# A decoder block's prologue: the order of modulation sums, low parts, squares and loads on VectorE, ScalarE and the load queue

## The chip, the cores and the metric

The kernel runs on one core of one Trainium2 chip. The metric is the time of one execution in microseconds (us), as the device measures it. A core has TensorE (PE in the profile; its weight loads are PEld), VectorE (DVE), ScalarE (ACT), GpSimd (POOL) and SyncE (SP), which here only issues DMA loads. Each engine works through its own queue in order.

## The reference

One layer over 1024 tokens of 1024 channels, all in float32:

```python
mod = jax.nn.silu(c) @ w_ada + b_ada
shift, scale, gate = jnp.split(mod, 3, axis=-1)
h = rms_norm(x, norm_gain) * (1.0 + scale[:, None, :]) + shift[:, None, :]
proj = h @ w_in
q, k, v, z_a, u, z_b, m_a, m_b = jnp.split(proj, offs, axis=-1)
p_a = (stick_breaking_attention(q, k, v) * silu(z_a)) @ w_branch_a
p_b = (multiscale_causal_pool(u, pool_w, pool_scale) * silu(z_b)) @ w_branch_b
out = x + gate * ((sigmoid(m_a) * p_a + sigmoid(m_b) * p_b) @ w_out)
```

A final RMS norm follows. What matters here is the first part: the modulation (shift and scale) from `c`, the normalised and modulated `h`, and the projection `u`, whose weights are multiplied beforehand with the pooling maps `pool_w`.

## The kernel before

**Precision.** To multiply in something close to float32, most operands are held as two parts: a high part, rounded to the fast matmul type by a ScalarE cast, and a low part, the rest, from a VectorE subtraction. A product then takes three matmuls: high by high, high by low, low by high.

**The prologue, about the first 80 us.** It works on the first half of the tokens (four row blocks of x, `x0` to `x3`) and makes for each of the eight 128-channel blocks `kb` a column of `h`, transposed, while it also makes the weights of `u`.

- `norm_x(sb)` (L239): ScalarE squares a row block and sums it (`junk`), GpSimd takes the power -1/2 (`st`, L245), VectorE scales the row block.
- `modulation(kb)` (L262): VectorE multiplies a 1 MB block of `w_ada` (`wa`, three buffers) with silu(c), spread over all partitions (`scb`), in two instructions that also sum (`mj`, one for shift and one for scale; each is followed by a short read of the accumulator). Then `mods` adds the offsets: on VectorE for block 0, on ScalarE for the others.
- `turn_x(sh, kb)` (L283): four TensorE transposes of x into a PSUM bank (`xt`).
- `make_h(sh, kb)` (L288): ScalarE applies shift and scale (`hf`), casts the high part (`hT`), and VectorE subtracts for the low part (also `hT`).
- `mapped(g, q)` (L322): TensorE multiplies a quarter of `u`'s weights with the map of group g (`wm`; below m00 to m13 for g 0 and 1, m20 to m23 for g 2), ScalarE casts the high part, VectorE takes the low part (`wg`). For groups 0 and 1 the operands are plain float32; for 2 and 3 the operands are split first by `split_map` (`phl`) and `split_half` (`wt`).
- The loop over `kb` (L391): TensorE multiplies block `kb` of `h` with the finished weights into four, later six accumulators (`ua`): two matmuls each on the high part, then the transposes of block `kb + 2`, then one matmul each on the low part.

PSUM has eight banks in four pairs (`pj`, `z`, `av`, `tr`). The accumulators take the banks that m10 to m13 leave, and so wait for the low parts of these; m20 to m23 and the transposes share `av` and `tr`.

**What sets the order.** From L361 to L437 `pinned` is set, and each engine's instructions keep the order in which the program gives them. All of these pass through the helper `order` (L93), so that their line in the profile is L95. Loads by `load` (L230) keep their order on the SP queue in any case (L231); a load that reuses a buffer waits at the head of that queue, with all later loads behind it. After L437 (the rest of `u`, the second half's `h`, the values, the pooling branch) the builder chooses the order by its own estimate of times; the attention (from L800) is pinned again.

The order on VectorE in the loop is: both sums of block `kb + 2`, then, when ScalarE has made its high part from them, the low part of block `kb + 2`, then the sums of the next block.

Of the kernel before, what the change touches and what calls it, by code (L numbers as in the profile page):

```python
# [9 lines left out]
F32 = mybir.dt.float32  # L10
# [33 lines left out]
LOAD_WO = (0, 0, 0, 1, 1, 2, 2, 2)  # L44

WHOLE, G2 = 2, 1
EPS = 1e-6
WINDOWS = (2, 4, 8, 16)

# [4 lines left out]
def block_kernel(ctx, tc, a, out):  # L54
# [12 lines left out]
    def bank(tag, name):  # L67
        return psp.tile([P, 512], F32, tag=tag, bufs=BANKS[tag], name=name)
# [24 lines left out]
    def order(op):  # L93
        def issue(*args, **kw):
            ins = op(*args, **kw)  # L95
            if pinned[0]:
                tc.keep_in_program_order(ins)
        return issue
# [99 lines left out]
    with pool("init") as init:  # L198
# [9 lines left out]
        nc.sync.dma_start(crow, a["c_row"])  # L208
        scb = init.tile([P, D], F32, name="scb")

        crows = [bank("tr", f"crow{hf}") for hf in range(2)]
        for hf in range(2):
            mm(crows[hf], ones[0:1, :], crow[:, hf * 512:hf * 512 + 512], start=True, stop=True)

        def spread():
            for hf in range(2):
                sigb = init.tile([P, 512], F32, tag="hf", bufs=2, name=f"sigb{hf}")
                order(act.activation)(sigb, crows[hf], AF.Sigmoid)
                order(v.tensor_mul)(scb[:, hf * 512:hf * 512 + 512], crows[hf], sigb)
# [16 lines left out]
                xs.extend([pr[:, 0], pr[:, 1]])  # L236
            load(xs[sb], a["x"][sb * P:(sb + 1) * P, :])

        def norm_x(sb, meanwhile=None):  # L239
            st = init.tile([P, 4], F32, tag="st", bufs=4, name=f"st{sb}")  # L240
            junk = init.tile([P, D + 1], F32, tag="junk", bufs=1, name=f"junk{sb}")[:, :D + (sb < 4)]
            order(act.activation)(junk, xs[sb] if sb > 3 else xe[sb], AF.Square, scale=D ** -0.5, accum_out=st[:, 0:1])
            if sb > 3:
                gp.tensor_scalar(st[:, 0:1], st[:, 0:1], 1.0, EPS, op0=ALU.mult, op1=ALU.add)
            gp.tensor_tensor(st[:, 2:3], st[:, 0:1], mhalf[:, 0:1], op=ALU.pow)  # L245
            if meanwhile:
                meanwhile()

            for cl in ((slice(0, P), slice(P, D)) if sb in (2, 3) else (slice(0, D),)):
                order(v.tensor_scalar_mul)(xs[sb][:, cl], xs[sb][:, cl], st[:, 2:3])  # L250

        was = {}

        def load_mod(kb, parts=(slice(0, 2),)):
            if kb not in was:
                was[kb] = init.tile([P, 2, D], F32, tag="wa", bufs=3, name=f"wa{kb}")
            for i in parts:
                load(was[kb][:, i].rearrange("p k c -> p (k c)"), a["w_mod"][kb][:, i.start * D:i.stop * D])
# [3 lines left out]
        def modulation(kb, parts_=(0, 1)):  # L262
            wa = was[kb]
            if kb not in accs_m:
                accs_m[kb] = init.tile([P, 2], F32, tag="acc", bufs=2, name=f"acc{kb}")
            acc = accs_m[kb]
            for i in parts_:
                vj = init.tile([P, D], F32, tag="vjunk", bufs=1, name=f"mj{kb}_{i}")
                order(v.scalar_tensor_tensor)(vj, wa[:, i], 1.0, scb, ALU.mult, ALU.mult, accum_out=acc[:, i:i + 1])
                if kb == 0 and i == 0:  # L270
                    order(v.tensor_add)(mod[0][:, 0:1], acc[:, 0:1], bada_v[:, 0:1])
                elif kb == 0:
                    order(v.scalar_tensor_tensor)(mod[0][:, 1:2], acc[:, 1:2], gain_v[:, 0:1], affb[:, 0:1], ALU.mult, ALU.add)
                elif i == 0:
                    order(act.activation)(mod[kb][:, 0:1], acc[:, 0:1], AF.Identity, bias=bada_v[:, kb:kb + 1])
                else:
                    order(act.activation)(mod[kb][:, 1:2], acc[:, 1:2], AF.Identity, bias=affb[:, kb:kb + 1], scale=gain_v[:, kb:kb + 1])
            if parts_[-1] == 1:
                del was[kb]
# [3 lines left out]
        def turn_x(sh, kb):  # L283
            pt = xts[sh, kb] = bank(("tr", "av")[kb % 2], f"xt{sh}_{kb}")
            for i in range(4):
                transpose(pt[:, i * P:(i + 1) * P], xs[4 * sh + i][:, kb * P:(kb + 1) * P])

        def make_h(sh, kb, lo_eng):  # L288
            hf = init.tile([P, 512], F32, tag="hf", bufs=2, name=f"hf{sh}_{kb}")
            order(act.activation)(hf, xts.pop((sh, kb)), AF.Identity, bias=mod[kb][:, 0:1], scale=mod[kb][:, 1:2])  # L290
            sl = slice(sh * 512, sh * 512 + 512)
            order(act.copy)(h_hi[:, kb, sl], hf)
            order(lo_eng.tensor_sub)(h_lo[:, kb, sl], hf, h_hi[:, kb, sl].bitcast(F32))

        NA = 6
# [26 lines left out]
        def mapped(g, q, tag):  # L322

            if g not in wg:
                wg[g] = first.tile([P, 2, KB, 256], F32R, tag="wg", bufs=4, name=f"wg{g}")
            ps = bank(tag, f"wm{g}_{q}")
            th, ml = halves[g, q // 2], maps[g]
            for e in range(2):
                ks = slice((2 * q + e) % 4 * P, (2 * q + e) % 4 * P + P)

                pairs = [(th[:, cb, ks], ml[:, cb]) for cb in range(2)] if g < WHOLE else [
                    (th[:, i, cb, ks], ml[:, j, cb]) for i, j in ((0, 0), (0, 1), (1, 0)) for cb in range(2)]
                for n, (l, r) in enumerate(pairs):
                    mm(ps[:, e * 256:e * 256 + 256], l, r, start=n == 0, stop=n == len(pairs) - 1)

            def out():
                dst = wg[g][:, :, 2 * q:2 * q + 2].rearrange("p i k d -> p i (k d)")
                order(act.copy)(dst[:, 0], ps)
                order(v.tensor_sub)(dst[:, 1], ps, dst[:, 0].bitcast(F32))
            return out  # L340

        def parts(i):
# [15 lines left out]
        load_x(3)  # L358
        load_half(1, 1, t1[:, 1])
        load_mod(1)  # L360
        pinned[0] = True  # L361
        spread()
        outs = [mapped(0, 0, "pj")]
        outs.pop()()
        outs.append(mapped(0, 1, "pj"))
        norm_x(0)
        outs.pop()()
        mapped(0, 2, "z")()
        norm_x(1)
        mapped(0, 3, "z")()  # L370
        modulation(0, (0,))
        norm_x(2)
        mapped(1, 0, "pj")()
        modulation(0, (1,))
        outs.append(mapped(1, 1, "pj"))
        norm_x(3, outs.pop())
        outs.append(mapped(1, 2, "z"))
        turn_x(0, 0)
        make_h(0, 0, v)
        outs.append(mapped(1, 3, "z"))  # L380
        for out_ in outs:
            out_()
        turn_x(0, 1)
        modulation(1)
        make_h(0, 1, v)
        whl = {i: parts(i) for i in range(4)}
        accs = [bank(tags[i], f"ua{i}") for i in range(4)]
        h = (h_hi, h_lo)
        sl = slice(0, 512)

        for kb in range(KB):  # L391
            if kb + 2 < KB:
                load_mod(kb + 2)
            if kb == G2:
                load_map(2)
                for hf in range(2):
                    load_half(2, hf)
            new = kb == G2 + 3
            if new:
                for i in (4, 5):  # L400
                    whl[i] = parts(i)
                    accs.append(bank(tags[i], f"ua{i}"))
            todo = [(i, k) for i in range(len(accs)) for k in range(0 if i > 3 and new else kb, kb + 1)]
            for n, (i, k) in enumerate(todo):
                mm(accs[i], whl[i][0][:, k], h_hi[:, k, sl], start=k == 0, stop=False)
                mm(accs[i], whl[i][1][:, k], h_hi[:, k, sl], start=False, stop=False)
            if kb + 2 < KB:
                turn_x(0, kb + 2)
            for i, k in todo:
                mm(accs[i], whl[i][0][:, k], h_lo[:, k, sl], start=False, stop=k == KB - 1)  # L410
            if kb + 2 < KB:
                modulation(kb + 2)
                make_h(0, kb + 2, v)
            if kb == G2:
                split_map(2)
                for hf in range(2):
                    split_half(2, hf)
            if kb in (G2 + 1, G2 + 2):
                for q in (0, 1):
                    mapped(2, 2 * (kb - G2 - 1) + q, ("av", "tr")[q])()  # L420
            if kb == KB - 3:
                load_map(3)
                for hf in range(2):
                    load_half(3, hf)
                for sb in range(4, 8):
                    load_x(sb)
            if kb == KB - 2:
                split_map(3)
                for hf in range(2):
                    split_half(3, hf)  # L430
                for sb in range(4, 8):
                    norm_x(sb)
        for q in range(4):
            mapped(3, q, ("av", "tr")[q % 2])()
        for i in (6, 7):
# [520 lines left out]
```

## Time and profile before

| | |
|---|---|
| median of three runs | 1235.88 us (1234.64 to 1236.06) |
| the profiled execution | 1235.22 us, its span 1233.2 us |
| mean granted TensorE clock | 0.996 |
| TensorE busy | 1212.8 us, 98% of the span |
| VectorE, ScalarE, GpSimd busy | 797.6, 561.8, 202.4 us |

The profile is of one execution. The page gives busy time by engine, the timeline lists instructions with their start and length in us and, in brackets, the idle time of the engine before them and what ended it. A table by stretches gives busy us of each engine, the share of the clock that TensorE was granted (PEclk), the mean busy share of the 16 DMA engines and the rate of their transfers. A matmul's record lasts longer than its share of a stream of matmuls, since they overlap; the step from start to start is the cost in a stream.

### The profile page before, as it was taken

What the parts mean: (1) busy time and instruction counts of PE and PEld (TensorE: products, weight loads), DVE (VectorE), ACT (ScalarE), POOL (GpSimd) and SP (SyncE); (2) the same over time, 40 slices, a digit from 0 to 9 for tenths busy, and PEclk for the clock granted to TensorE, in tenths of its full rate; (3) what the DMA queues carried; (4) which work ended last, traced back from release to release, by engine and by line L of the source; (5) the groups of instructions that cost most, each with busy time, mean ns of one, the idle gap of its engine ahead of it and who ended that gap; (6) DMA issues with size and microseconds to landing.
All of it is one profiled execution on the core that took longest, in us unless ns stands there. A gap on an engine that the chain in (4) does not pass through costs nothing.

```text
span 1233.2 us, 16089 instructions
## 1 busy us (share of the span) xinstructions
PE 1212.8 (98%) x5760; PEld 1004.9 (81%) x5760; DVE 797.6 (65%) x1076; ACT 561.8 (46%) x1047; POOL 202.4 (16%) x365
## 2 busy tenths in 40 slices
PE   8899999999999999999999999999999999999997
PEld 5787888888888888888888888888888888888886
DVE  5644485476610297786878778688786863585654
ACT  4446333234301356566656556666666553232111
POOL 1010000000222342312313122222222310001001
PEclk9899999999999999999999999999999999999999
DMA  8635999425953321233423224231333225995612
GB/s 336 213 134 191 330 369 365 147 80 174 330 166 126 129 67 39 70 124 103 128 93 107 71 98 128 95 120 57 94 125 103 95 90 169 335 321 169 201 65 86
DMA packets 72803, 192.44 MB, mean 156 GB/s; under 512 B 7698, under 2 KB 21010, under 8 KB 70804
## 3 DMA queue, kind: packets, MB, share of 16 engines
q1 hardware_dynamic: 61956, 172.28, 40.7%
q10 hardware_dynamic: 10768, 19.14, 4.7%
q8 instruction: 45, 0.74, 0.2%
q14 instruction: 34, 0.28, 0.1%
HBM read 136.86 MB, written 50.34 MB: 152 GB/s over the span
## 4 chain that ended last, share of the span: by engine, by line
PE 83%; issue 6%; DVE 6%; POOL 2%; DMA 1%; ACT 1%; POOLq 0%; SPq 0%; DVEq 0%; ACTq 0%
PE p L95 27%; PE pb L95 7%; PE pa L95 7%; PE wzb L95 7%; PE v L95 7%; PE o L95 6%; PE u L95 4%; PE av L95 4%; PE z L95 4%; PE wt L95 4%; PE ua L95 2%; PE wm L95 2%; DVE om L689 2%; DVE be L690 2%; DMA gr<-ga_d 1%
## 5 line engine op out<-in xcount | busy, mean ns | idle before, releaser
L95 PE MATMUL p<-hT,w 128*128 128x512 f32 x1920 | 534.8, 399 | 0.3 <-ACT m_sg L184 0.3
L95 PEld LDWEIGHTS p<-hT,w 128*128 128x128 f32 x1920 | 341.5, 188 | 56.7 <-ACT m_sg L184 0.7
L689 DVE TENSOR_TENSOR_SCAN om<-om 128x512 f32<-128x512 f32 (+7 forms) x128 | 175.2, 1369 | 52.2 <-POOL om L687 29.0
L682 ACT ACTIVATE om<-z 128x512 f32<-128x512 f32 (+2 forms) x192 | 94.3, 491 | 103.8 <-PE z L95 101.9
L709 DVE TENSOR_TENSOR wt<-wt,wt 128x512 fp32r<-128x512 f32 (+1 forms) x160 | 100.9, 631 | 45.2 <-ACT wt L708 43.9
L687 POOL TENSOR_SCALAR_AFFINE_SELECT om<-om 128x128 f32<-128x128 f32 x128 | 67.5, 527 | 328.3 <-ACT om L682 302.2
L708 ACT CAST wt<-wt 128x512 fp32r<-128x512 f32 (+1 forms) x160 | 87.2, 545 | 68.6 <-PE wt L95 64.9
L690 DVE TENSOR_TENSOR be<-be,om 128x511 f32<-128x511 f32 (+7 forms) x128 | 101.6, 793 | 11.2 <-DVE om L689 0.9
L95 PEld LDWEIGHTS wt<-ident,be 128*128 128x128 f32 x576 | 72.0, 140 | 28.1 <-DVE wt L709 3.3
L95 PE MATMUL av<-wt,vv 128*128 128x512 f32 x320 | 94.2, 375 | 0.0
L683 ACT ACTIVATE be<-z 128x512 f32<-128x512 f32 (+2 forms) x192 | 93.6, 487 | 0.0
L95 PE MATMUL wt<-ident,be 128*128 128x128 f32 x576 | 89.1, 272 | 4.2 <-DVE wt L709 4.1
L95 PE MATMUL o<-wo,mhl 128*128 128x512 f32 (+2 forms) x408 | 90.2, 379 | 0.0
L95 PE MATMUL pa<-ga,wa 128*128 128x512 f32 x384 | 88.8, 389 | 0.0
L95 PE MATMUL pb<-gb,wb 128*128 128x512 f32 x384 | 87.2, 389 | 0.0
L95 PE MATMUL v<-wv,hT 128*128 128x512 f32 x384 | 87.2, 389 | 0.0
L95 PE MATMUL wzb<-hT,wzb 128*128 128x512 f32 x384 | 87.2, 389 | 0.0
L95 PEld LDWEIGHTS o<-wo,mhl 128*128 128x128 f32 x408 | 74.6, 188 | 14.1
L95 PEld LDWEIGHTS pa<-ga,wa 128*128 128x128 f32 x384 | 72.1, 188 | 14.9
L95 PEld LDWEIGHTS v<-wv,hT 128*128 128x128 f32 x384 | 72.1, 188 | 15.0
L95 PEld LDWEIGHTS wzb<-hT,wzb 128*128 128x128 f32 x384 | 72.1, 188 | 15.0
L95 PEld LDWEIGHTS pb<-gb,wb 128*128 128x128 f32 x384 | 72.1, 188 | 15.0
(124 smaller groups left out, 1430.6 us busy)
## 6 DMA issues: line engine op xcount, KB each, us to landing
w_raw<-in_w_in SPq DMA_DIRECT2D x40, 512.0 KB, 4.4
l_raw<-in_w_in SPq DMA_DIRECT2D x32, 512.0 KB, 5.7
wl_d<-l_raw SPq DMA_DIRECT2D x32, 512.0 KB, 4.0
w<-wl_d SPq DMA_DIRECT2D x32, 512.0 KB, 3.8
v_d<-vo SPq DMA_DIRECT2D x16, 512.0 KB, 5.5
vv<-v_d SPq DMA_DIRECT2D x8, 1024.0 KB, 5.6
wa_raw<-in_w_branch_a SPq DMA_DIRECT2D x16, 512.0 KB, 5.6
wa<-in_w_mod SPq DMA_DIRECT2D x7, 1024.0 KB, 4.9
```

The source lines that it names most:

```text
L95: ins = op(*args, **kw)
L682: act.activation(om[:, b0:b0 + n], zp[:, :n], AF.Sigmoid, scale=-0.125)
L683: act.activation(be[:, b0:b0 + n], zp[:, :n], AF.Sigmoid, scale=0.125)
L687: gp.affine_select(out=tl[:, :P], in_=tl[:, :P], pattern=[[1, P]], compare_op=ALU.is_gt, fill=fill, base=0, channel_multiplier=-1)
L689: v.tensor_tensor_scan(om[:, :W], om[:, :W], om[:, :W], 1.0, ALU.mult, ALU.min)
L690: v.tensor_mul(be[:, 1:W], be[:, 1:W], om[:, :W - 1])
L708: act.copy(wt[:, 0, :off], pt[:, :off])
L709: v.tensor_sub(wt[:, 1, :off], pt[:, :off], wt[:, 0, :off].bitcast(F32))
```

## The change

In the pinned prologue, the orders are rewritten:

- `norm_x` is parted into `square_x` and `scale_x`, and squares and scalings are placed one by one. The squares of x0 and x1 come before the casts of m00 and m02. Scaling and the sums of block 0 take other places among the low parts of m00 to m11.
- `make_h` can leave its low part to a new function `low_h`. Block 1's sums come in front of block 0's low part and of the low parts of m12 and m13; in the loop the sums of block `kb + 2` come in front of the low part of block `kb + 1`.
- Loads of `wa` are written behind the sums that free their buffer: block 2 before the pinned part, block 3 behind block 0's sums, followed by the loads of map 2, and block `kb + 5` behind the sums of block `kb + 2`. The loads of map 3 stand at `kb == 3` (were at 5), those of x4 to x7 at `kb == 6` (were at 5). The sequence of the loads among each other stays.
- Two matmuls of the ones by the identity (`BUSY = 2`) go into a PSUM bank that nobody reads, ahead of TensorE's first matmuls, which spread `c` over the partitions (`crow`).

The diff, cut to its core:

```diff
+        idle = bank("av", "idle")
+        for _ in range(BUSY):
+            mm(idle[:, :P], ones, ident, start=True, stop=True)
...
+        def low_h(sh, kb, lo_eng):
+            hf, sl = lows.pop(kb), slice(sh * 512, sh * 512 + 512)
             order(lo_eng.tensor_sub)(h_lo[:, kb, sl], hf, h_hi[:, kb, sl].bitcast(F32))
...
+        load_mod(2)
         pinned[0] = True
+        hi, lo_ = (0,), (1,)
         spread()
...
+        m00 = mapped(0, 0, "pj")
+        square_x(0)
+        m00(hi)
+        m00(lo_)
+        m01 = mapped(0, 1, "pj")
+        m01(hi)
+        scale_x(0)
+        m01(lo_)
+        m02 = mapped(0, 2, "z")
+        square_x(1)
+        m02()
+        scale_x(1)
+        m03 = mapped(0, 3, "z")
         modulation(0, (0,))
+        m03()
+        square_x(2)
+        m10 = mapped(1, 0, "pj")
+        m10(hi)
+        m11 = mapped(1, 1, "pj")
         modulation(0, (1,))
+        load_mod(3)
+        load_map(2)
+        for hf in range(2):
+            load_half(2, hf)
+        square_x(3)
+        scale_x(2, slice(0, P))
+        m10(lo_)
+        m11(hi)
+        scale_x(3, slice(0, P))
+        m11(lo_)
+        m12 = mapped(1, 2, "z")
         turn_x(0, 0)
+        scale_x(2, slice(P, D))
+        scale_x(3, slice(P, D))
+        make_h(0, 0, None)
+        m13 = mapped(1, 3, "z")
         turn_x(0, 1)
+        m12(hi)
         modulation(1)
+        load_mod(4)
+        low_h(0, 0, v)
+        m12(lo_)
+        m13(hi)
+        m13(lo_)
+        make_h(0, 1, None)
...
             if kb + 2 < KB:
                 turn_x(0, kb + 2)
+                modulation(kb + 2)
+                if kb + 5 < KB:
+                    load_mod(kb + 5)
+            if kb + 1 < KB:
+                low_h(0, kb + 1, v)
             for i, k in todo:
                 mm(accs[i], whl[i][0][:, k], h_lo[:, k, sl], start=False, stop=k == KB - 1)
             if kb + 2 < KB:
-                modulation(kb + 2)
-                make_h(0, kb + 2, v)
+                make_h(0, kb + 2, None)
```

More of the change, by code (lines that the diff above doesn't have):

```diff
@@ L46 @@
 WHOLE, G2 = 2, 1
+BUSY = 2
 EPS = 1e-6
@@ L237, in load_x, with square_x @@
             load(xs[sb], a["x"][sb * P:(sb + 1) * P, :])
-        def norm_x(sb, meanwhile=None):
-            st = init.tile([P, 4], F32, tag="st", bufs=4, name=f"st{sb}")
+        stats = {}
+        def square_x(sb):
+            st = stats[sb] = init.tile([P, 4], F32, tag="st", bufs=4, name=f"st{sb}")
             junk = init.tile([P, D + 1], F32, tag="junk", bufs=1, name=f"junk{sb}")[:, :D + (sb < 4)]
@@ L245, in norm_x, with scale_x @@
             gp.tensor_tensor(st[:, 2:3], st[:, 0:1], mhalf[:, 0:1], op=ALU.pow)
[L246 to L250, printed above, removed]
+        def scale_x(sb, cl=slice(0, D)):
+            order(v.tensor_scalar_mul)(xs[sb][:, cl], xs[sb][:, cl], stats[sb][:, 2:3])
         was = {}
@@ L292, in make_h @@
             order(act.copy)(h_hi[:, kb, sl], hf)
+            lows[kb] = hf
+            if lo_eng:
+                low_h(sh, kb, lo_eng)
+        lows = {}
+        def low_h(sh, kb, lo_eng):
+            hf, sl = lows.pop(kb), slice(sh * 512, sh * 512 + 512)
             order(lo_eng.tensor_sub)(h_lo[:, kb, sl], hf, h_hi[:, kb, sl].bitcast(F32))
@@ L334, in mapped, with out @@
                     mm(ps[:, e * 256:e * 256 + 256], l, r, start=n == 0, stop=n == len(pairs) - 1)
-            def out():
+            def out(which=(0, 1)):
                 dst = wg[g][:, :, 2 * q:2 * q + 2].rearrange("p i k d -> p i (k d)")
-                order(act.copy)(dst[:, 0], ps)
-                order(v.tensor_sub)(dst[:, 1], ps, dst[:, 0].bitcast(F32))
+                if 0 in which:
+                    order(act.copy)(dst[:, 0], ps)
+                if 1 in which:
+                    order(v.tensor_sub)(dst[:, 1], ps, dst[:, 0].bitcast(F32))
             return out
@@ L360, in block_kernel @@
         load_mod(1)
+        load_mod(2)
         pinned[0] = True
+        hi, lo_ = (0,), (1,)
         spread()
[L363 to L370, printed above, removed]
-        modulation(0, (0,))
-        norm_x(2)
-        mapped(1, 0, "pj")()
-        modulation(0, (1,))
-        outs.append(mapped(1, 1, "pj"))
-        norm_x(3, outs.pop())
-        outs.append(mapped(1, 2, "z"))
+        m00 = mapped(0, 0, "pj")
[11 more added lines that the diff above has]
+        m03 = mapped(0, 3, "z")
+        modulation(0, (0,))
+        m03()
[3 more added lines that the diff above has]
+        m11 = mapped(1, 1, "pj")
+        modulation(0, (1,))
+        load_mod(3)
[9 more added lines that the diff above has]
+        m12 = mapped(1, 2, "z")
         turn_x(0, 0)
[L379 to L382, printed above, removed]
+        scale_x(2, slice(P, D))
+        scale_x(3, slice(P, D))
+        make_h(0, 0, None)
+        m13 = mapped(1, 3, "z")
         turn_x(0, 1)
+        m12(hi)
         modulation(1)
-        make_h(0, 1, v)
+        load_mod(4)
[4 more added lines that the diff above has]
+        make_h(0, 1, None)
         whl = {i: parts(i) for i in range(4)}
@@ L391, in block_kernel @@
         for kb in range(KB):
[L392 to L397, printed above, removed]
             new = kb == G2 + 3
@@ L420, in block_kernel @@
                     mapped(2, 2 * (kb - G2 - 1) + q, ("av", "tr")[q])()
-            if kb == KB - 3:
+            if kb == 3:
                 load_map(3)
@@ L424, in block_kernel @@
                     load_half(3, hf)
+            if kb == KB - 2:
                 for sb in range(4, 8):
                     load_x(sb)
-            if kb == KB - 2:
                 split_map(3)
@@ L431, in block_kernel @@
                 for sb in range(4, 8):
-                    norm_x(sb)
+                    square_x(sb)
+                    scale_x(sb)
         for q in range(4):
```

## The prediction

> **What bounds the kernel now.** I read the page first, then busy time by stretches, the list of who waited for whom, the timeline of the first 80 us, and stretches again for the clock.
>
> ```profile
> span 1233.2 us, 16089 instructions
> ...
> PE 1212.8 (98%) x5760; PEld 1004.9 (81%) x5760; DVE 797.6 (65%) x1076; ACT 561.8 (46%) x1047; POOL 202.4 (16%) x365
> ```
>
> TensorE (PE) is busy 98% of the span, so an edit on other engines can only win where PE stands still or runs slowly. The stretches say where that is (us of the stretch, then busy us of each engine):
>
> ```profile
> core 0: us, PE busy (x) PEld busy (x) DVE busy (x) ACT busy (x) POOL busy (x), PEclk, DMA share, GB/s
> 0.00:10.00 10.00, 7.27 (x13) 4.03 (x14) 1.72 (x4) 2.69 (x4) 1.55 (x28) 1.00 0.75 266
> 10.00:25.50 15.50, 14.06 (x64) 11.97 (x63) 9.97 (x19) 9.48 (x17) 2.68 (x4) 1.00 0.98 381
> 25.50:33.00 7.50, 5.32 (x25) 3.83 (x24) 5.55 (x9) 2.67 (x6) 0.00 (x0) 0.97 0.91 340
> 33.00:40.00 7.00, 6.86 (x27) 4.97 (x26) 4.50 (x9) 2.83 (x7) 0.00 (x0) 0.79 0.52 178
> 40.00:50.00 10.00, 7.08 (x37) 6.41 (x38) 6.48 (x9) 6.31 (x11) 0.00 (x0) 0.83 0.41 134
> ```
>
> Between 10 and 50 us PE idles 1.44 + 2.18 + 0.14 + 2.92 = 6.7 us, and the granted clock drops. After that it has work all the time; the list of PE's waits from 80 to 420 us has one entry:
>
> ```profile
> PE u L95 <- ACT u_sg L191: 0.2, 1, 0.2
> ```
>
> So whatever brings PE sooner to where it is at 50 us should reach the end undiminished. What holds PE back is a loop through three engines, once per block (from the timeline):
>
> ```profile
> 31.36 0.69 DVE L95 TENSOR_TENSOR hT<-hf,hT 128x512 fp32r<-128x512 f32 x1 [1.91 <-ACT hT L95]
> ...
> 31.39 2.77 PE L95 MATMUL ua<-hT,wg 128*128 128x512 f32 x8 [2.18 <-ACT hT L95]
> 31.97 1.22 DVE L95 SCALAR_TENSOR_TENSOR mj<-wa,scb 128x1024 f32<-128x1024 f32 x1
> ...
> 33.23 1.23 DVE L95 SCALAR_TENSOR_TENSOR mj<-wa,scb 128x1024 f32<-128x1024 f32 x1
> ...
> 34.50 0.39 ACT L95 ACTIVATE mods<-acc,affb,vecs 128x1 f32<-128x1 f32 x1 [0.97 <-DVE mj L95]
> ...
> 34.92 0.78 ACT L95 ACTIVATE hf<-xt,mods 128x512 f32<-128x512 f32 x1
> 35.73 0.62 ACT L95 CAST hT<-hf 128x512 fp32r<-128x512 f32 x1
> 36.38 0.69 DVE L95 TENSOR_TENSOR hT<-hf,hT 128x512 fp32r<-128x512 f32 x1 [1.91 <-ACT hT L95]
> ```
>
> Low part (31.36), two modulation sums (31.97, 33.23), then ScalarE's three steps, then the next low part at 36.38: 5.02 us a block, of which VectorE (DVE) idles 1.91 because its next sums stand behind the low part that ScalarE has yet to feed. The clock follows PE's gaps:
>
> ```profile
> 10.00:12.00 2.00, 2.00 (x6) 1.64 (x5) 0.69 (x1) 1.63 (x3) 0.06 (x1) 1.00 1.07 410
> 14.00:16.00 2.00, 2.00 (x11) 1.75 (x10) 0.97 (x2) 1.30 (x2) 0.00 (x0) 1.00 1.03 418
> ...
> 22.36:25.77 3.41, 2.44 (x14) 2.19 (x15) 2.12 (x6) 2.04 (x4) 0.00 (x0) 1.00 0.83 308
> 29.18:32.60 3.42, 1.24 (x6) 1.04 (x6) 1.51 (x4) 1.78 (x3) 0.00 (x0) 1.00 0.77 256
> 32.60:36.01 3.41, 3.41 (x11) 2.74 (x11) 1.83 (x4) 1.74 (x4) 0.00 (x0) 0.50 0.57 156
> ...
> 42.84:46.25 3.41, 3.33 (x14) 3.04 (x15) 3.39 (x3) 0.94 (x1) 0.00 (x0) 0.50 0.23 94
> ```
>
> A stretch with PE busy 1.24 of 3.42 us is followed by one at 0.50; one with 2.44 of 3.41 is not. At the start the same matmuls go at 6 in 2 us around 11 us and 11 in 2 us around 15, so PE starts slow too.
>
> **The change, part by part.** *Prologue on DVE.* These rows carry it:
>
> ```profile
> 15.18 1.06 ACT L95 ACTIVATE junk<-x 128x1025 f32<-128x1025 f32 x1
> 15.31 0.69 DVE L95 TENSOR_TENSOR wg<-wm,wg 128x512 fp32r<-128x512 f32 x1 [1.03 <-ACT wg L95]
> ...
> 17.00 0.75 DVE L95 TENSOR_SCALAR x<-x,st 128x1024 f32<-128x1024 f32 x1 [0.99 <-POOL st L245]
> 17.66 0.68 DVE L95 TENSOR_TENSOR wg<-wm,wg 128x512 fp32r<-128x512 f32 x1
> ...
> 18.26 1.22 DVE L95 SCALAR_TENSOR_TENSOR mj<-wa,scb 128x1024 f32<-128x1024 f32 x1
> ...
> 19.86 1.03 POOL L245 TENSOR_TENSOR st<-st,mhalf 128x1 f32<-128x1 f32 x1 [1.18 <-ACT junk L95]
> ...
> 22.26 0.22 DVE L95 SCALAR_TENSOR_TENSOR mods<-acc,vecs,affb 128x1 f32<-128x1 f32 x1
> ...
> 23.33 0.33 PE L95 MATMUL xt<-ident,x 128*128 128x128 f32 x1 [1.44 <-DVE x L95]
> ...
> 26.96 1.21 DVE L95 SCALAR_TENSOR_TENSOR mj<-wa,scb 128x1024 f32<-128x1024 f32 x1
> ```
>
> The square of row block 1 (15.18) moves ahead of the third cast, into about 13.5; DVE's 0.99 wait before 17.00 goes. Walking the new queue by start-to-start steps (low 0.60, scaling 0.66, sum 1.25): low at 15.3, scaling 15.9, first sum 16.6 (was 18.26), low 17.9, second sum 18.5, its offset done at 20.0 (was 22.5). Then first part of x2, low, first part of x3 at 20.7 to 20.9 (20.9 if the GpSimd step again takes 1.03), low, the two rests, and block 1's first sum at 22.7 to 22.9, was 26.96: 4.2 us earlier. The transposes that waited 1.44 for x3 start at 21.4, as the matmuls ahead of them end. ScalarE's order from the third cast on is unchanged, so nothing there moves later. Its square of x0 now stands before the first cast, beside eight slow wm matmuls (2.7 us at 6 in 2 us) that the cast waits for anyway; should x0 land too late for that cover, the lateness is the cost.
>
> *New wait.* Low parts of the two last mapped tiles (m12, m13) now stand behind block 1's sums: 22.8 + 2 x 1.25 + low of h 0.60 + 0.69 = 26.6. PE has then issued the first two accumulators (24.9 by my walk) and idles about 1.6 us for the third's PSUM bank. It was not there before; it replaces the 1.44 and most of the 2.18.
>
> *The loop.* DVE's step is now two sums and a low part without the 1.91: 3.1 us. PE's is 12 matmuls of 0.23 (6.51 / 28, below) and 4 transposes of some 0.11 (at most 2.97 / 22, below), 3.2 us. So blocks 1 to 3 come at 3.2 instead of 5.0 us: block 1's matmuls at 28.9 (were 31.39), block 2's at 32.1, its low ones done at 35.3. Block 3's cast ends at 34.4: sums done 32.6, plus mods, hf, hT 1.9.
>
> *Map 2.* Splits keep their place behind that cast:
>
> ```profile
> 41.27 0.61 ACT L95 CAST phl<-praw 128x512 fp32r<-128x512 f32 x1
> ...
> 41.79 1.99 ACT L95 CAST wt<-wt_raw 128x1024 fp32r<-128x1024 f32 x2
> ...
> 42.86 2.36 DVE L95 TENSOR_TENSOR wt<-wt_raw,wt 128x1024 fp32r<-128x1024 f32 x2 [0.17 <-ACT wt L95]
> 42.88 4.82 PE L95 MATMUL wm<-phl,wt 128*128 128x256 f32 x24 [3.02 <-ACT wt L95]
> ...
> 50.90 3.09 PE L95 MATMUL wm<-phl,wt 128*128 128x256 f32 x24
> ...
> 53.82 6.51 PE L95 MATMUL ua<-hT,wg 128*128 128x512 f32 x28
> ```
>
> 34.35 + 0.52 + 1.04 gives 36.0 for the first half's high part: PE starts map 2 at 36.0, was 42.88, after 0.7 us of waiting instead of 3.02; four matmuls on it waits 0.8 for the half's low part (was 0.3). The 24 ran 4.82 us, mostly at half clock; at full clock 3.09, 1.7 less. Block 3 starts at 39.6, 8.0 us earlier. One us is given back: DVE must do block 4's sums (38.2 to 40.7) and a low part before it can lower m20, whose cast also follows block 4's on ScalarE (43.1); low at 43.8, while PE, done with block 3 at 42.8, wants that bank. The second 24 start at 43.9 instead of 50.90, and the 28 at 46.7 instead of 53.82: **7.1 us**. After that my walk finds margins of only 0.4 to 0.5 us (block 5's bank, m22's low part) but no wait; a miss costs about as much again.
>
> *Loads.* Their order on the SP queue is the same; only the release is earlier. The page's longest wait of that queue is for sums, and a 1 MB load takes
>
> ```profile
> wa<-in_w_mod SPq DMA_DIRECT2D x7, 1024.0 KB, 4.9
> ```
>
> 4.9 us from issue, or 2.75 at 381 GB/s back to back. Ten loads up to block 1's weights are 6.84 MB: 2.66 by 10 us (266 GB/s there), the rest by 21.0; block 2's by 23.7, block 3's by 26.5, map 2's by 29.9, block 4's by 32.7. Wanted at 22.8, 27.0, 30.1, 35 and 38.2: hidden, by 1.8 us at the closest. Gone by that cover, each us late is a us on DVE and on PE.
>
> *Two extra matmuls* on TensorE before the first: four passes of 128 columns, nearest row the transposes' 0.11, twice that at half clock, so 0.9 in all. They lie in PE's first idle 2.7 us (10.00 - 7.27), before the row of c lands, and can start only when their operands are made; bounds: nothing, or the whole 0.9 late. I take nothing, the nearer end, because the idle time is three times as long. A gain is a rival, below.
>
> *Clock.* My gaps of 1.6 and of 0.7 + 0.8 leave stretches of 3.4 us with PE busy 1.9, between the two rows that decide. I take full clock; a half-clock stretch would cost 0 around 30 us, where the walk has slack, and 0.8 to 1.3 around 40 to 45.
> [...]
>
> *Sum.* The profiled execution took 1235.2 (span 1233.2 and 2.0 around it); minus 7.1 is 1228.1. The median of the runs, 1235.88, lies 0.7 higher: **1228.8**.
>
> **The rivals.** *Earlier clock.* PE reports work from 2.73 us but is slow until about 12. If the extra full-array matmuls bring the release a 3.4 us stretch sooner, eight wm matmuls go at 0.22 instead of 0.43: 1.7 more, 1227.1. Against: 0.9 us is a quarter of a stretch.
> [...]
>
> *Half the gain.* Two half-clock stretches (2 us) and the two thin margins (1 us) leave 4: 1232. For: three short gaps close together. Against: the 2.44 row.
>
> *No change.* The DMA engines or a later stage absorb it: 1235 or so. Against: PE waits 0.2 us in 80 to 420; loads there start as buffers come free, so they move along.
>
> *Slower.* From line 437 the order is not pinned; the builder chooses it, and may choose anew after a changed prologue.
>
> ```profile
> 93.47 2.97 PE L95 MATMUL xt<-ident,x 128*128 128x128 f32 x22
> ```
>
> There eight blocks of transposes, each with hf, hT and a low part behind it (0.78 + 0.62 + 0.69 = 2.1 us), lie beside u matmuls. Were these issued first, eight blocks would wait 2.1 - 0.44 each, 13 us: 1242. It decides from five uncovered blocks on; the page shows every one covered today.
>
> **How the numbers follow.** Forecast 0.62, earlier clock 0.12, half the gain 0.14, no change 0.08, slower 0.04. About 0.2% (2.5 us) is what a measurement can tell from no change, so faster is 0.62 + 0.12 + 0.14 = 0.88, same 0.08, slower 0.04. The range takes in 1227.1 less the 1.4 us by which the runs differ, and the half gain: 1225.6 to 1232.0; outside it lie the last two and a tail.
>
> **What would show it.** Right: first sum of block 1 at about 22.8; DVE's waits for hT gone until the splits; PE waiting some 1.6 us near 25 and 1 us near 43; map 2 at 36 and 44; third map's matmuls at 69.4 instead of 76.5; granted clock 1.00 from about 12 on. Wrong: sums that wait for weights, half-clock stretches after 25 us, or new PE waits past 50 us.

## The result and the profile after

| | before | after |
|---|---|---|
| median | 1235.39 us (1234.64 to 1236.06, 4 runs) | 1228.06 us (1227.15 to 1228.42, 4 runs) |
| profiled execution, its span | 1235.22, 1233.2 us | 1228.19, 1226.2 us |
| mean granted clock | 0.996 | 0.999 |

The ratio is 0.994, with a 95% interval of 0.9922 to 0.9957: 7.3 us faster, where 7.1 were forecast (1228.8). When both kernels were measured once more, the ratio was 0.9936 (0.9922 to 0.9949).

The page of the profile after, to be held against the one before: TensorE (PE) does the same work and four matmul records more (x5764, was x5760); it is busy for 1.8 us less, in a span that is 7.0 us shorter.

```profile
span 1226.2 us, 16097 instructions
...
PE 1211.0 (99%) x5764; PEld 1003.3 (82%) x5764; DVE 796.8 (65%) x1076; ACT 561.7 (46%) x1047; POOL 202.8 (17%) x365
```

The stretches are those of the prediction:

```profile
0.00:10.00 10.00, 8.40 (x16) 4.95 (x17) 1.72 (x4) 2.78 (x5) 1.56 (x28) 1.00 0.74 250
10.00:25.50 15.50, 15.33 (x69) 12.64 (x67) 12.14 (x23) 9.97 (x20) 2.21 (x4) 1.00 1.02 410
25.50:33.00 7.50, 6.57 (x32) 5.27 (x33) 7.43 (x13) 4.68 (x11) 0.00 (x0) 1.00 1.02 407
33.00:40.00 7.00, 6.21 (x41) 5.13 (x40) 4.88 (x6) 3.97 (x6) 0.00 (x0) 1.00 0.53 215
40.00:50.00 10.00, 9.17 (x54) 7.76 (x53) 6.37 (x12) 5.81 (x11) 0.00 (x0) 1.00 0.82 305
```

PE's idle time between 10 and 50 us falls from 6.7 to 0.17 + 0.93 + 0.79 + 0.83 = 2.7 us, and in this execution the clock column reads 1.00 in all of these stretches (the last figure but two of each row), where the kernel before has 0.97, 0.79 and 0.83 between 25.5 and 50 us. VectorE (DVE) is busy 7.43 of the 7.5 us from 25.5 to 33, where it was busy 5.55: its queue no longer stands still there. The list of PE's waits in the first 80 us names the places that are left; its first entry is the start, ahead of the two extra matmuls:

```profile
PE idle L96 <- POOL x L232: 1.6, 1, 1.6
PE ua L96 <- DVE wg L96: 1.1, 1, 1.1
PE wm L96 <- DVE wg L96: 0.8, 1, 0.8
PE wm L96 <- DVE wt L96: 0.5, 1, 0.5
PE wm L96 <- ACT wt L96: 0.3, 1, 0.3
```

The other four are the waits of the forecast's walk, which has 1.6, 1.1, 0.8 and 0.7 us for them: the listed waits are 0.3 to 0.5 shorter. Most of that is the way of counting, since a record runs on past the issue of the next matmul (four `ua` matmuls take 1.17 us by their records and 4 x 0.23 in a stream). In the timeline the loop reads as follows; the columns are start, length, engine, line, operation, operands, count, and in brackets the idle time before.

```profile
22.67 1.22 DVE L96 SCALAR_TENSOR_TENSOR mj<-wa,scb 128x1024 f32<-128x1024 f32 x1
...
26.43 1.33 PE L96 MATMUL ua<-hT,wg 128*128 128x512 f32 x4 [1.08 <-DVE wg L96]
...
26.89 1.22 DVE L96 SCALAR_TENSOR_TENSOR mj<-wa,scb 128x1024 f32<-128x1024 f32 x1
...
28.15 1.23 DVE L96 SCALAR_TENSOR_TENSOR mj<-wa,scb 128x1024 f32<-128x1024 f32 x1
...
29.30 0.69 DVE L96 TENSOR_TENSOR hT<-hf,hT 128x512 fp32r<-128x512 f32 x1
...
29.90 1.22 DVE L96 SCALAR_TENSOR_TENSOR mj<-wa,scb 128x1024 f32<-128x1024 f32 x1
```

From sum to sum it is 29.90 - 26.89 = 3.0 us, with no idle time in between; it was 5.0. Behind the loop PE's timeline has the two halves of map 2 and the start of map 3:

```profile
35.80 0.74 PE L96 MATMUL wm<-phl,wt 128*128 128x256 f32 x4 [0.27 <-ACT wt L96]
...
43.71 3.08 PE L96 MATMUL wm<-phl,wt 128*128 128x256 f32 x24 [0.83 <-DVE wg L96]
...
69.41 3.02 PE L96 MATMUL wm<-phl,wt 128*128 128x256 f32 x24
```

The row of map 3 in the kernel before:

```profile
76.56 3.02 PE L95 MATMUL wm<-phl,wt 128*128 128x256 f32 x24
```

What the walk forecast and what the trace has, in us (the first row is an end, the others are starts):

| | before | forecast | after |
|---|---|---|---|
| offset of block 0's second sum done | 22.48 | 20.0 | 19.98 |
| block 1's first sum | 26.96 | 22.7 to 22.9 | 22.67 |
| map 2, first half | 42.88 | 36.0 | 35.80 |
| map 2, second half | 50.90 | 43.9 | 43.71 |
| first matmul of map 3 | 76.56 | 69.4 | 69.41 |

So 7.15 us are won by 70 us of 1226, and 7.0 are left at the end. From map 3 on all four computing engines issue the same instructions in the same order in both profiles, and PE's lead stays between 6.6 and 7.2 us. The order that the builder chooses has not changed, and no later stage took the gain back.

### The profile page after: what moved, and what is told of

It reads as the page before. It is cut to its first block, busy times and chain, and to the rows that moved or that the text cites. A ratio compares the mean times of both kernels' runs of the same rounds, so it can differ in the third digit from the quotient of the medians.

```text
span 1226.2 us, 16097 instructions
## 1 busy us (share of the span) xinstructions
PE 1211.0 (99%) x5764; PEld 1003.3 (82%) x5764; DVE 796.8 (65%) x1076; ACT 561.7 (46%) x1047; POOL 202.8 (17%) x365
## 4 chain that ended last, share of the span: by engine, by line
PE 81%; DVE 7%; issue 7%; POOL 2%; DMA 1%; ACT 1%; POOLq 0%; SPq 0%; DVEq 0%; ACTq 0%
PE p L96 29%; PE v L96 7%; PE pa L96 7%; PE pb L96 7%; PE o L96 6%; PE u L96 4%; PE wzb L96 4%; PE av L96 4%; PE wt L96 4%; PE z L96 4%; PE ua L96 2%; DVE om L727 2%; DVE be L728 2%; PE wm L96 1%; POOL om L725 1%
```

## The experiments

My theory (order theory): the gain is DVE's queue alone. In the prologue its sums come 4.2 us sooner, in the loop they no longer stand behind a low part that ScalarE has yet to feed. Rivals: the clock (the half-clock stretches of before are gone), the two extra matmuls, and the place of the loads. Within the prologue the moves were not tried one by one: how much of its part comes from the squares on ScalarE and how much from the sums on DVE is not shown by a run of its own.

**One part alone.** The loop's order put into the kernel before:

```diff
             if kb + 2 < KB:
                 turn_x(0, kb + 2)
+                modulation(kb + 2)
+            if kb > 0 and kb + 1 < KB:
+                low_h(0, kb + 1, v)
...
-                modulation(kb + 2)
-                make_h(0, kb + 2, v)
+                make_h(0, kb + 2, None)
```

> The kernel before, with the loop's order of the change alone: the sums of block kb + 2 stand ahead of the low part of block kb + 1; the prologue, the loads and the first matmuls are as before. Order theory (the gain comes from DVE's queue, part by part): block 1 still starts at 31.4 us, blocks 2 and 3 come sooner, because DVE no longer waits 1.9 us in front of the sums of block 3 and of block 4's neighbours; map 2 starts at about 40.5 instead of 42.9, its second half at 48.4 instead of 50.9: 2.6 us faster than before. Rival, clock theory (the gain is the half clock that goes away): PE still stands still 2.2 us before block 1, so one half-clock stretch stays, and the gain is what the other one cost, 1.7 us. Rival, loads or extra matmuls: 0.

Measured: 1232.02 us beside 1235.12, ratio 0.9974 (0.9963 to 0.9984): 3.1 us faster. The reverse, the change with the old order in the loop:

```diff
-        make_h(0, 1, None)
+        make_h(0, 1, v)
...
                 turn_x(0, kb + 2)
-                modulation(kb + 2)
-                if kb + 5 < KB:
-                    load_mod(kb + 5)
-            if kb + 1 < KB:
-                low_h(0, kb + 1, v)
...
-                make_h(0, kb + 2, None)
+                modulation(kb + 2)
+                if kb + 5 < KB:
+                    load_mod(kb + 5)
+                make_h(0, kb + 2, v)
```

> The change with the loop's order taken back: squares, scalings, sums and low parts up to the loop are as in the change, in the loop the low part of block kb + 2 stands behind the sums of that block, as before. Order theory: block 1's matmuls at 28.9 instead of 31.4 us, then the old step of 5.0 us a block, so map 2 starts at about 39.0 and its second half at 47.0: 4.0 us faster than before, and with the loop's 2.6 nearly the whole 7.1 (the rest, 0.5, is what the two do together). Rival, loop theory (only the loop's 1.9 us a block matter, what is won ahead of it is lost again in waits for weights): 0 to 1 us faster. Rival, clock theory: PE stands still over 3 us before map 2 as it did, so that half-clock stretch stays; the other one goes, 1.7 us.

Measured: 1231.40 us, ratio 0.997 (0.9959 to 0.9982): 3.7 us faster. PE's timeline with the loop's order alone, and then with the prologue's alone:

```profile
40.23 0.73 PE L95 MATMUL wm<-phl,wt 128*128 128x256 f32 x4 [0.52 <-ACT wt L95]
...
48.14 3.12 PE L95 MATMUL wm<-phl,wt 128*128 128x256 f32 x24 [0.84 <-DVE wg L95]
```

```profile
38.45 5.90 PE L96 MATMUL wm<-phl,wt 128*128 128x256 f32 x24 [3.00 <-ACT wt L96]
...
47.39 3.00 PE L96 MATMUL wm<-phl,wt 128*128 128x256 f32 x24
```

Map 2 starts where the order theory had it, within 0.6 us (40.5 and 39.0), and so does its second half (48.4 and 47.0). The parts nearly add up: 3.1 + 3.7 = 6.8 of 7.3 us.

In the second run's profile the clock does cost something. Map 2's first half ran at half clock (0.50 from 37.40 to 44.22 us), 5.90 us instead of 3.00. DVE's low part of m20, which the second half waits for in the other profiles, was done early enough:

```profile
45.74 1.28 DVE L96 TENSOR_TENSOR wg<-wm,wg 128x512 fp32r<-128x512 f32 x2
```

The first of the two ends at about 46.4, but PE, which had no idle time since 38.45, came to the second half only at 47.39, 0.9 us later. From half to half it is 8.9 us here, 7.9 in the run with the loop's order alone (8.0 in the kernel before). Map 3 starts 2.70 us sooner than before in the first run's trace and 3.58 in the second's, together 6.3 of the 7.15 of the change; 0.9 is what is missing.

**The clock by itself.** The kernel before, its clock kept up by extra matmuls in its two long waits:

```diff
             ps = bank(tag, f"wm{g}_{q}")
+            if (g, q) == (2, 0):
+                for _ in range(13):
+                    mm(ps[:, :P], ones, ident, start=True, stop=True)
...
+            if kb == 1:
+                warm = bank("av", "warm")
+                for _ in range(9):
+                    mm(warm[:, :P], ones, ident, start=True, stop=True)
```

> The kernel before, with extra matmuls of the ones by the identity, whose results are overwritten or never read, in PE's two long waits: 9 before block 1 (2.0 us) and 13 before map 2 (2.8 us). The granted clock should stay at 1.00 from 12 us on. Clock theory: the two half-clock stretches cost PE 1.7 us each, and at least the second of them counts, so 1.5 us faster than before or more. Order theory: after the second stretch PE waits for DVE's low part of m20, which stands behind block 4's sums whatever the clock, so map 2's first half ends 1.6 us sooner, PE waits that much longer before the second half at 50.9, and the time is as before within 0.3 us. This tells whether the 1.7 us that my sum booked under the clock was really in it.

Measured: 1235.48 us beside 1235.12, ratio 1.0002 (0.9993 to 1.001): no gain, and the interval leaves room for 0.9 us at most. The clock was kept (two stretches of this run; the clock is the third figure from the end), and PE's timeline says where the gain went:

```profile
41.83:45.24 3.41, 2.77 (x22) 2.38 (x21) 3.23 (x4) 1.52 (x2) 0.00 (x0) 1.00 0.38 161
45.24:48.65 3.41, 3.41 (x23) 3.01 (x22) 1.93 (x4) 1.64 (x4) 0.00 (x0) 1.00 0.31 38
```

```profile
43.71 2.62 PE L95 MATMUL wm<-phl,wt 128*128 128x256 f32 x20 [0.53 <-DVE wt L95]
46.16 1.99 PE L95 MATMUL ua<-hT,wg 128*128 128x512 f32 x8
...
50.48 3.08 PE L95 MATMUL wm<-phl,wt 128*128 128x256 f32 x24 [0.96 <-DVE wg L95]
```

Block 3 starts at 46.16 instead of 47.54, 1.4 us sooner, and then PE waits 0.96 us, where it had not waited, for the low part that DVE makes behind block 4's sums. The second half starts at 50.48, was 50.90. So the clock theory falls for the kernel before: DVE is the later of the two there, though by little, since PE was 0.25 us ahead of it even with its half-clock stretch (four `ua` matmuls from 49.72, at 0.23 each, end at 50.65). In the run with the prologue alone, where map 2's whole first half ran at half clock, PE was the later one.

**The extra matmuls.**

```diff
-BUSY = 2
+BUSY = 0
```

> The change without its two extra matmuls on TensorE. My theory: same time as the change within 0.2 us, full clock again from about 12 us on, since the extra matmuls fill a quarter of a stretch of 3.4 us only. Rival (they bring the clock's release forward in some executions): 1 to 1.7 us slower in the median than the change, and a wider spread.

Measured: 1227.43 us, ratio 0.9937 (0.9925 to 0.9949). The change itself, run once more, has 0.9936, so the extra matmuls are worth nothing that can be told.

> The change itself, once more, on the same chip as the next two runs, to compare them within one call: 0.994 of the kernel before, 1228 us.

Measured: 1227.45 us, ratio 0.9936 (0.9922 to 0.9949), beside 1235.04 for the kernel before.

**The loads.** First their place in the program, undone:

```diff
-        load_mod(2)
...
-        load_mod(3)
-        load_map(2)
-        for hf in range(2):
-            load_half(2, hf)
...
-        load_mod(4)
...
+            if kb + 2 < KB:
+                load_mod(kb + 2)
+            if kb == G2:
+                load_map(2)
+                for hf in range(2):
+                    load_half(2, hf)
...
-                if kb + 5 < KB:
-                    load_mod(kb + 5)
```

(map 3 and x4 to x7 go back in the same way.)

> The change with the loads written at their old places in the program. Theory that the place in the program is nothing, since the sequence on the load queue is the same and each load waits for its own buffer: same time as the change within 0.2 us, block 3's weights issued at about 20 us all the same. Rival (a load written ahead of the sums waits for more than its buffer): up to 2.7 us slower, the load of a block being that long.

Measured: 1227.82 us, ratio 0.9941 (0.9929 to 0.9954), 0.4 above the change beside it, with ranges that overlap (1227.08 to 1229.39 and 1227.04 to 1227.78). In its trace block 3's weights are issued at 19.4 us, in the change's at 19.8. So the place in the program is worth nothing that can be told. Then the margin, by 1 MB more on the queue:

```diff
         load_half(1, 1, t1[:, 1])
+        for i in range(2):
+            load(wl_d[i], a["w_in"][tiles[i]])
         load_mod(1)
```

> The change with two copies of 512 KB from memory to memory (into a part of a scratch tensor that nothing uses) on the load queue ahead of block 1's weights. They take some 2.7 us of the DMA engines. My theory, loads hidden by 1.7 us at the closest: block 1's weights land at 23.7 instead of 21.0, DVE's first sum of block 1 starts about 1.1 us later than the 22.7 of the change, and the later loads stay hidden, so the time is 1.1 us over the change's. Rival, loads not near at all (their landing is earlier than I read it): 0. Rival, the prologue is bound by its loads throughout: 2.7 us slower than the change.

Measured: 1228.87 us, ratio 0.9956 (0.9943 to 0.9968), 0.8 over the first 1228.06 of the change and 1.4 over its 1227.45. DVE's timeline shows the wait that the change is free of:

```profile
23.85 1.23 DVE L96 SCALAR_TENSOR_TENSOR mj<-wa,scb 128x1024 f32<-128x1024 f32 x1 [1.50 <-DMA wa<-in_w_mod]
```

The sum starts at 23.85 instead of 22.67, 1.2 us later, where 1.1 were expected, and no later sum of the loop waits for weights. PE then stands still for 3.0 us instead of 1.1, and the clock column has 0.50 from 28.26 to 31.67 us in this profile, with PE busy 0.65 of 3.41 us in the stretch ahead of it. Still map 2's second half starts only 1.4 us later than in the change, 0.2 more than the sum. By these figures loads are hidden in the change by some 1.5 us (2.7 less 1.2), not more.

**A version beyond.** The waits that are left stand around map 2's split. It is drawn apart:

```diff
                 turn_x(0, kb + 2)
+                if kb == G2:
+                    low_map, low_0 = split_map(2), split_half(2, 0)
                 modulation(kb + 2)
...
                 low_h(0, kb + 1, v)
+            if kb == G2 + 1:
+                low_1()
...
             if kb == G2:
-                split_map(2)
-                for hf in range(2):
-                    split_half(2, hf)
+                low_map()
+                low_0()
+                low_1 = split_half(2, 1)
```

(`split_map` and `split_half` make the high part and return a function for the low one.)

> The change with the split of map 2 drawn apart: the casts of the map and of its first half stand ahead of block 3's mods on ScalarE (instead of behind block 3's cast), their low parts behind low part 2 as now, and the low part of the second half behind the sums and the low part that follow. Theory that DVE's queue from 33 to 43 us sets the last wait (block 4's sums stand behind three low parts, the first of which waits 1.8 us for ScalarE): DVE's sums of block 4 start at 34.7 instead of 38.1, PE finds map 2 ready at 35.3 and its second half's bank free when it comes there at about 41.3 instead of 43.7: 2.3 us faster than the change. Rival, PE is the bound by then and its waits of 0.3, 0.5 and 0.8 us are all there is: at most 1.6 us faster. Rival, the loads of map 2 come too late for it (they land at 26 to 29 us): no gain.

Measured: 1224.80 us, ratio 0.992 (0.9906 to 0.9934).

> The run with the earlier split, without the two extra matmuls. If these are worth nothing, as the run without them said, it gives the 2.3 to 2.6 us that the earlier split gave against the change, so 1225.5 us; if they do bring the clock's release forward in some executions, it is up to 1 us slower than that.

Measured: 1224.81 us, ratio 0.9915 (0.9901 to 0.9928), beside the change's 1227.45: 2.6 us better. It and the next version, which are alike in time, are the fastest. DVE's timeline, then PE's, of this run:

```profile
33.41 1.22 DVE L96 TENSOR_TENSOR wt<-wt_raw,wt 128x1024 fp32r<-128x1024 f32 x1
34.54 1.22 DVE L96 SCALAR_TENSOR_TENSOR mj<-wa,scb 128x1024 f32<-128x1024 f32 x1
```

```profile
35.26 3.00 PE L96 MATMUL wm<-phl,wt 128*128 128x256 f32 x24
...
41.30 3.00 PE L96 MATMUL wm<-phl,wt 128*128 128x256 f32 x24
```

Block 4's sums start at 34.5 (38.06 in the change), map 2's halves at 35.3 and 41.3 without a wait. PE's list of waits from 20 to 80 us has one entry left, the 1.3 us at 25. To take that one away as well:

```diff
         m12(hi)
-        modulation(1)
-        load_mod(4)
-        low_h(0, 0, v)
-        m12(lo_)
         m13(hi)
-        m13(lo_)
+        modulation(1, (0,))
+        m12(lo_)
+        modulation(1, (1,))
+        load_mod(4)
+        m13(lo_)
+        low_h(0, 0, v)
```

> As the run with the earlier split, and in the prologue the low part of m12 stands between the two sums of block 1 and that of m13 behind them, ahead of block 0's low part. This takes away the new wait (PE standing still at 25 us, 1.1 us in the change) and costs the second sum 0.6 us. If that wait is worth anything by then, block 1 starts at 28.2 instead of 28.7 and the time is 0.4 to 0.5 us below the run with the earlier split alone. Rival, DVE's sums bound the loop and not PE: 0, or 0.6 us slower.

Measured: 1224.54 us, ratio 0.9919 (0.9905 to 0.9932), the same as the split alone. My expectation was wrong here, and DVE's timeline says why:

```profile
24.69 0.69 DVE L96 TENSOR_TENSOR wg<-wm,wg 128x512 fp32r<-128x512 f32 x1 [0.67 <-ACT wg L96]
...
26.43 0.69 DVE L96 TENSOR_TENSOR wg<-wm,wg 128x512 fp32r<-128x512 f32 x1
```

The cast of m12 stands behind block 0's two steps on ScalarE, so DVE now waits 0.67 us for it between the sums, and PE's wait (0.9 us in this run) moves on to the next accumulator, which m13's low part frees.

**c's row on the whole array.** The change, with 127 rows of zeros around the row:

```diff
-        crow = init.tile([P, D], F32, tag="vjunk", bufs=1, name="crow")[0:1]
-        nc.sync.dma_start(crow, a["c_row"])
+        crow = init.tile([P, D], F32, tag="vjunk", bufs=1, name="crow")
+        v.memset(crow, 0.0)
+        act.dma_start(crow[0:1], a["c_row"])
...
-            mm(crows[hf], ones[0:1, :], crow[:, hf * 512:hf * 512 + 512], start=True, stop=True)
+            mm(crows[hf], ones, crow[:, hf * 512:hf * 512 + 512], start=True, stop=True)
```

> The change with c's row on TensorE as a matmul of 128 rows, 127 of them zero, instead of one row: the same number of matmuls and columns, but the whole array is in use from the start. It needs a fill by DVE and the load goes by ScalarE's queue, so c is there perhaps 0.5 us later. Theory that one-row matmuls do not count for the clock: full clock one stretch of 3.4 us earlier, at 7 to 10 us instead of 10 to 12, eight matmuls of map 0 at 0.22 instead of 0.43 us, so 1.7 less 0.5: about 1 us faster than the change. Rival, the clock's release has nothing to do with the rows: release as before, 0 to 0.5 us slower.

Measured: 1228.88 us, ratio 0.9954 (0.9941 to 0.9966), 0.8 slower than the change's first 1228.06. This run settles nothing about the rows: c landed late, and its matmuls start at 5.8 us, not at 2.75 as in the change. The stretch from 5.02 to 8.44 us has PE busy 2.65 of 3.42 us; 8 matmuls stand in the one up to 11.85 and 17 in the one behind it, so full clock came at 11.9.

## Why the prediction was right, step by step

- *The place* (PE stands still only before 50 us, and what is won there reaches the end): shown. 7.15 us at map 3 became 7.0 at the end of the span, with the same order of instructions behind it. With that the rivals "no change" and "slower" fall.
- *The prologue on DVE*, 4.2 us: block 1's first sum came 4.3 sooner. The prologue alone gave 3.7 us in the time, against 4.0 expected. Its moves were only tried together.
- *The loop*, 5.0 to 3.2 us a block: 3.0 to 3.2 measured. The loop alone gave 3.1 us, against 2.6 expected.
- *The new wait* at 25 us: there, 1.1 us by the list. I had not said what it is worth at the end; moving it to the next accumulator gained nothing, so its worth stays open.
- *Given back at map 2*, about 1 us: 0.8 by the list. That it was DVE's queue, and not PE, is shown by the earlier split, which won 2.6 us by order alone.
- *Loads hidden by 1.8 us*: near. The extra megabyte, 2.7 us of load by the walk's rate, made DVE 1.2 us late, which leaves 1.5. (The walk counts ten loads up to block 1's weights; there are thirteen on the queue, and its 6.84 MB are right.)
- *The square of x0 under cover of the first cast*: the cover was thin, and it did not hold in every execution. In the first profile of the change ScalarE waited for x0, and the first cast came at 10.96 instead of 10.23:

```profile
9.90 1.06 ACT L96 ACTIVATE junk<-x 128x1025 f32<-128x1025 f32 x1 [2.74 <-DMA x<-in_x]
...
10.96 0.57 ACT L96 CAST wg<-wm 128x512 fp32r<-128x512 f32 x1
```

  The prediction would have charged that lateness; it cost nothing, since DVE's second low part starts at 13.57, was 13.59. When the change was profiled again, the square began at 8.96 and the cast at 10.28, behind PE's matmuls as planned. The 2.7 us for the eight matmuls were too short: in the traces they start 0.43 apart, 3.4 us in all.
- *The extra matmuls at nothing*: shown within the noise. The rival that gave them 1.7 us falls: full clock comes at 12.0 us in the change's profile, with them, and at 12.1 in the kernel before, without; in the time it is 1227.45 us with them and 1227.43 without.
- *The clock*: I booked 1.7 us of map 2's gain to it on the way to block 3's 8.0, and took 1 us back behind it. The end of the walk was right, and this item was not a term of it: the kernel before gains nothing from a full clock (1235.48 us beside 1235.12). The end is set by DVE (block 4's sums, a low part, m20's low part), in both kernels; the half-clock stretches of before lay beside that, with 0.25 us to spare at map 2's second half. The rival "half the gain" did not come about because no half-clock stretch follows in the prologue: the clock column reads 1.00 from 12.0 us on through the prologue in the change's profile. Its price is not refuted: in the run with the prologue alone two such stretches in a row cost 0.9 us.

## What to carry to other kernels

In a queue that is worked in order, put what waits for nobody ahead of what waits for another engine: here two sums of 1.25 us each moved in front of a low part, and a step of three engines went from 5.0 to 3.0 us. Before a half-clock stretch is booked as a loss, ask what the engine waits for behind it; a run that keeps the clock up costs a few lines. Here two single stretches cost nothing that can be told in the kernel before (1235.48 us with the clock kept up, 1235.12 without), and two in a row cost 0.9 us in the run with the prologue alone. And when the order is mended, look at the next wait's own queue: another 2.6 us lay in the split that had kept its place.

## What the runs showed of the hardware

In the profile of the kernel before, the granted clock changes at 32.60, 36.01, 42.84 and 46.25 us, that is 3.41, 6.83 and 3.41 us apart. Full clock came at 12.1 us there (9 matmuls in the 3.41 us ahead of it, 17 in the 3.42 behind), at 12.0 in the change's profile (9 and 17), at 11.9 in the run with c on 128 rows (8 and 17) and at 10.1 in the run with the prologue alone (9 and 17). Stretches of this last run:

```profile
3.26:6.67 3.41, 3.41 (x5) 0.87 (x4) 0.69 (x1) 0.70 (x2) 0.00 (x0) 1.00 1.04 348
6.67:10.09 3.42, 3.42 (x9) 2.70 (x10) 0.69 (x1) 0.97 (x2) 0.00 (x0) 1.00 0.91 340
10.09:13.50 3.41, 3.41 (x17) 3.02 (x16) 2.04 (x3) 2.09 (x5) 0.56 (x1) 1.00 1.01 405
33.99:37.40 3.41, 1.46 (x9) 0.94 (x7) 1.50 (x3) 2.38 (x6) 0.00 (x0) 1.00 0.54 142
37.40:40.81 3.41, 2.32 (x9) 2.03 (x10) 3.23 (x5) 1.95 (x3) 0.00 (x0) 0.50 0.52 216
40.81:44.22 3.41, 3.41 (x18) 3.41 (x18) 2.36 (x4) 1.24 (x3) 0.00 (x0) 0.50 0.11 12
44.22:47.63 3.41, 3.41 (x20) 2.86 (x20) 2.50 (x4) 1.82 (x4) 0.00 (x0) 1.00 0.89 311
```

The clock column says 1.00 from the start, but the counts do not: 9 matmuls in the stretch from 6.67, 17 in the one from 10.09. The stretch from 3.26 (PE busy 3.41 us, mostly with the one-row matmuls of c) is followed by the one with 9, the stretch from 6.67 (busy 3.42 us, with wm) by the one with 17. The stretch with 1.46 busy us of 3.41 is followed by one at 0.50, that with 2.32 by another at 0.50, and the full one by one at 1.00. So in this run PE's gap of 3.00 us ahead of map 2 came with two stretches at 0.50. In the kernel before, the stretch with 2.44 is followed by one at 1.00, and so is one with 2.07 in the run with c on 128 rows:

```profile
25.51:28.93 3.42, 2.07 (x9) 1.14 (x8) 3.42 (x6) 2.17 (x5) 0.00 (x0) 1.00 1.06 410
28.93:32.34 3.41, 3.41 (x20) 2.85 (x19) 3.38 (x7) 1.86 (x4) 0.00 (x0) 1.00 0.91 329
```

Yet at the very end of the run without the extra matmuls a stretch with 2.75 is followed by one at 0.50:

```profile
1216.44:1219.85 3.41, 2.75 (x25) 2.60 (x23) 2.83 (x8) 0.00 (x0) 0.00 (x0) 1.00 0.00 0
1219.85:1223.27 3.42, 0.00 (x0) 0.00 (x0) 1.21 (x6) 0.72 (x1) 0.55 (x1) 0.50 0.24 90
```

So the busy share of a stretch does not decide by itself, and no threshold follows from these rows. Whether the single row of c's matmuls is why the stretch from 3.26 is followed by a slow one is not shown: the run made to test it did not settle it.
